# TensorE products that take their moving operand in 64-byte pieces from two halves, beside shifted tiles

## The chip, the cores and the metric

One core of one Trainium2 chip runs the whole program. The metric is the device time of one execution in microseconds (us). Terms used below: the PE is the matrix engine (TensorE); a product on it has a *stationary* operand of 128 x 128 weights, which a weight load (PEld in the profile) puts in place, and a *moving* operand of 128 partitions x 256 or 512 columns, which is streamed from SBUF past the weights; the result goes to PSUM. While one product streams, the weights of the next one are loaded. DVE, ACT and POOL are the vector, scalar and GpSimd engines.

## The reference

One encoder block over 512 tokens of width 2048, in float32. What matters here is that nearly all of it is matrix products:

```
proj  = rmsnorm(x) @ w_in                    # 512x2048 @ 2048x11280
...     # short convolution; hyena: two long convolutions by FFT (products with DFT tables)
...     # mLSTM, 4 heads, both directions, in chunks of 128
mixed = sigmoid(gate_a) * (y_a @ w_branch_a) + sigmoid(gate_b) * (y_b @ w_branch_b)
x     = x + mixed @ w_out                    # 512x2048 @ 2048x2048
gu    = rmsnorm(x) @ w_gate_up               # 512x2048 @ 2048x11264
x     = x + (silu(gu[:, :5632]) * gu[:, 5632:]) @ w_down
out   = rmsnorm(x)
```

## The kernel before, in words

Each float32 operand is split in two numbers of the type float32r: `h`, rounded, and `l`, the rest. One product of the reference becomes three on the PE (`mm3`): high by high, high by low, low by high. ACT makes `h` by a cast, DVE makes `l` by a subtraction (lines 74 to 80, 165 to 171, 1067 to 1072). All of these products go through one helper, `mm` (line 68), so the profile gives them one line, L69. The names in a row of the profile are output, then moving operand, then stationary operand: in `mm<-wh,h` the weights' high part `wh` is streamed and the activation's `h` is stationary; in `mm<-a,wh` it is the other way round. `mm` and `sd` are the two pools of PSUM tiles, four banks of 512 columns each.

The stages follow each other, with these products:

- To about 857 us: columns of `w_in` in groups (`group_feat`, 512 columns, moving operand `a`), with the hyena and mLSTM work in between (tiles `g` and `sg`, mostly 256 columns), and the values (`group_v`, 256 columns).
- To about 1157 us and again from about 1546 to 2402 us: the merge gates and the gate and up columns. These are Winograd (Strassen-like) products of 2 x 2 blocks: seven products of eight steps in place of eight, each step three products of 256 columns, so one column of blocks is 7 x 8 x 3 = 168 products. There are 16 + 44 = 60 such columns. The moving operands are halves of the tiles `a` or combinations `T`; the DVE forms the weights' sums `s`, and evacuates the results.
- From about 1157 to 1546 us: branch A (`ya`, tiles `a`), branch B (`yb`, tiles `y`), 384 products of 512 columns each, then the output projection, mostly with 512 columns.
- From about 2402 us: the down projection (`group_tok`), 512 columns, the weights moving and `h` stationary.

By the loops of the code there are 11,904 products of 256 columns: 60 x 168 = 10,080 in the Winograd columns, 4 x 192 = 768 for the values, 2 x 192 = 384 in the last two half groups of the output projection, 672 for the long convolutions. And 5,952 of 512 columns: 24 x 96 = 2,304 in feature groups, 32 for the gates, 768 in the branches, 3 x 192 = 576 for the output projection, 44 x 4 x 4 x 3 = 2,112 for the down projection, 96 for the mLSTM scores, 64 for the filters. The rest are transposes and small products.

The order of work on each engine is the order in which the code issues it (`drive` and `turns` interleave the streams by fixed rates). Tiles live in pools that are stacked from the left and from the right end of SBUF, so a pool's size sets the address of what is stacked after it. Most tiles are 2048 bytes in each partition; the tiles `g` are 2 x 258 words and so start at many distances. On the left come the small constants (`cp`), the weights (`wp`), the activations `a` (`ap`) and later `ts`, `pg`, the `w2...` pools and the tiles of the down projection; on the right `pr`, then `sx`, the `wm...` pools, `py` (tiles `y`) and `tp` (tiles `T` of the gate and up columns).

Of the kernel before, what the change touches and what calls it, by code (L numbers as in the profile page):

```python
# [8 lines left out]
F32 = mybir.dt.float32  # L9
# [6 lines left out]
P = 128  # L16
# [18 lines left out]
def hybrid_block_kernel(ctx, tc, x, norm1_w, w_in, conv_w, conv_b, filt_w1, filt_b1, filt_freq1,  # L35
# [6 lines left out]
    def new(pool, tag, shape=(P, L), dt=F32):  # L42
        n_tile[0] += 1
        return pool.tile(list(shape), dt, tag=tag, name=f"{tag}_{n_tile[0]}")
# [7 lines left out]
    cp = ctx.enter_context(tc.tile_pool(name="cp", bufs=1))  # L52
    wp = ctx.enter_context(tc.tile_pool(name="wp", bufs=1))
    wpool = [wp]
    WB = [4]
    ap_cm = tc.tile_pool(name="ap", bufs=32)
    ap = ap_cm.__enter__()
# [7 lines left out]
    def sd_ps():  # L65
        return new(psd, "sd")

    def mm(o, a, b, start, stop):
        nc.tensor.matmul(o, a, b, start=start, stop=stop)  # L69

    def mm3(o, aH, aL, bH, bL, start, stop):
        mm(o, aH, bH, start, False)
        mm(o, aH, bL, False, False)
        mm(o, aL, bH, False, stop)
# [44 lines left out]
    def dram(name, shape=(P, L)):  # L119
        return dp.tile(list(shape), F32, tag=name, name=name)  # L120
# [44 lines left out]
    def split_w(src, shape):  # L165
        n_tile[0] += 1
        h = wpool[0].tile(shape, F32R, tag="wh", name=f"wh_{n_tile[0]}", bufs=WB[0])
        l = wpool[0].tile(shape, F32R, tag="wl", name=f"wl_{n_tile[0]}", bufs=WB[0])
        nc.scalar.copy(h, src)  # L169
# [374 lines left out]
    h2 = {}  # L544
# [431 lines left out]
    def stream_a():  # L976
        yield from gate_rows()
        yield from need("filter")
        for kind, n in (("hy", 0), ("hy", 1), ("hd", 0), ("hy", 2), ("hy", 3)):
            yield from hyena(n) if kind == "hy" else mlstm(n)  # L980
        ph_cm.__exit__(None, None, None)
        ts_pool.append(ts_cm.__enter__())
        done.add("ts")
        for h in (1, 2, 3):
            yield from mlstm(h, h + 1)

    def stream_b():
        yield from filter_net()
        done.add("filter")
        yield from spectra()  # L990
        yield from need("ts")
        yield from combos_x()

    def turns(*streams):


        streams = [[s, 0] for s in streams]
        while streams:
            for _ in range(len(streams)):
                s = streams.pop(0)  # L1000
                if s[1] > tick[0]:
                    streams.append(s)
                    continue
                r = next(s[0], "end")
                if r == "pause":
                    s[1] = tick[0] + PAUSE
                if r != "end":
                    streams.append(s)
                if not isinstance(r, str):
                    break  # L1010
            else:
                r = "wait"
            if streams:
                yield r
# [139 lines left out]
    side = turns(stream_b(), stream_a())  # L1154
# [35 lines left out]
        return sx.tile(list(shape), F32, tag="bt", name=f"bt_{n_tile[0]}", bufs=4)  # L1190

    wm_cm = {t: tc.tile_pool(name="wm" + t, bufs=b, side="right", reuse_waits="tile") for t, b in (("r", 4), ("s", 6), ("h", 2), ("l", 2))}
    wm = {t: cm.__enter__() for t, cm in wm_cm.items()}
    d_g = [[dram(f"d_g{k}_{b}") for b in range(16)] for k in range(2)]

    def wtile(tag, shape, dt, bufs):
# [37 lines left out]
            nc.scalar.activation(C[j], C[j], AF.Sigmoid)  # L1234
            nc.gpsimd.dma_start(dst[j], C[j])

    for t in ("l", "h", "s", "r"):
        wm_cm[t].__exit__(None, None, None)
    ts_cm.__exit__(None, None, None)
    pg_cm = tc.tile_pool(name="pg", bufs=20, reuse_waits="tile")  # L1240
# [124 lines left out]
    for c in range(3):  # L1365
# [10 lines left out]
    hs = ctx.enter_context(tc.tile_pool(name="hs", bufs=3, reuse_waits="tile"))  # L1376
    w2_cm = {t: tc.tile_pool(name="w2" + t, bufs=b, reuse_waits="tile")
             for t, b in (("tb", 7), ("s2", 6), ("ta", 7), ("r2", 4), ("h2", 1), ("l2", 1))}
    w2 = {t: cm.__enter__() for t, cm in w2_cm.items()}

    def wt2(tag, shape, dt):
        return new(w2[tag], tag, shape, dt)
# [29 lines left out]
            nc.vector.tensor_tensor(U[j], U[j], G[j], ALU.mult)  # L1412
            nc.gpsimd.dma_start(d_h[f + j], U[j])

    for cm in reversed(list(w2_cm.values())):
        cm.__exit__(None, None, None)
    tp_cm.__exit__(None, None, None)
    sx_cm.__exit__(None, None, None)
# [48 lines left out]
    for c in range(4):  # L1467
        t = new(xq, "xst")
# [14 lines left out]
    for tb in range(4):  # L1483
        ts = slice(tb * P, (tb + 1) * P)
        for c in range(4):
# [3 lines left out]
            t = x2[tb][c]  # L1489
# [7 lines left out]
        for c in range(4):  # L1497
            t = x2[tb][c]
# [64 lines left out]
```

## Time and profile before

| | |
|---|---|
| median of 3 runs | 2893.94 us (2892.57 to 2894.06) |
| profiled execution | 2893.9 us, its span 2892.2 us |
| PE busy | 2864.4 us (99%), 18,412 products |
| weight loads (PEld) busy | 2593.9 us (90%) |
| DVE busy | 2107.6 us (73%) |
| ACT busy | 1271.4 us (44%) |
| DMA | 377.01 MB, 130 GB/s |

How to read it: PE rows have one record for each product, from its start to its modelled end. A new product starts before the one ahead has left the array, so records overlap: a 512-column product has a record of about 390 ns, while one starts every 227 ns or so. The price of a product is therefore the distance between starts, or the length of a stretch with nothing but products divided by their count. The chain of waits in order of time gives such stretches: start, length, line and count.

### The profile page before, as it was taken

How to read it: one execution, taken by the hardware profiler on the slowest of the kernel's cores; microseconds unless marked ns; L12 is line 12 of the kernel's file. 1: busy time of each engine (PE TensorE's matmuls, PEld its weight loads, DVE VectorE, ACT ScalarE, POOL GpSimd, SP SyncE). 2: the span in 40 equal slices, each digit the busy share in tenths (PEclk: the TensorE clock that was granted, in tenths of full speed). 3: DMA queues.
4: the chain of work that ended last, by engine and by line, in shares of the span. 5: the costliest groups of instructions: out<-in, count | busy, mean ns of one | idle time of the engine just before them, and what ended most of it. 6: DMA issues, size and time to landing. Idle time of an engine off the chain costs nothing.

```text
span 2892.2 us, 48205 instructions
## 1 busy us (share of the span) xinstructions
PE 2864.4 (99%) x18412; PEld 2593.9 (90%) x18412; DVE 2107.6 (73%) x3844; ACT 1271.4 (44%) x2265; POOL 187.6 (6%) x431
## 2 busy tenths in 40 slices
PE   9999999999999999999999999999999999999998
PEld 7788887888889999888899999999999998888886
DVE  7897978789578888554549888898888985233336
ACT  5434354346645455222435444444444445233224
POOL 0101011112200001000110000000000000000000
PEclk9999999999999999999999999999999999999999
DMA  5334333334444444743443433343343336343333
GB/s 179 110 121 128 120 117 124 117 118 145 132 146 128 131 142 139 247 139 95 152 148 109 130 120 114 120 125 118 117 128 114 118 110 207 96 131 117 124 114 127
DMA packets 285589, 377.01 MB, mean 130 GB/s; under 512 B 18620, under 2 KB 222852, under 8 KB 285357
## 3 DMA queue, kind: packets, MB, share of 16 engines
q1 hardware_dynamic: 261339, 298.36, 33.2%
q0 software_dynamic: 22752, 73.44, 7.5%
q8 instruction: 144, 2.36, 0.3%
q10 hardware_dynamic: 1266, 2.13, 0.2%
q14 instruction: 88, 0.72, 0.1%
HBM read 326.67 MB, written 47.20 MB: 129 GB/s over the span
## 4 chain that ended last, share of the span: by engine, by line
PE 82%; DVE 2%; DMA 1%; issue 0%; ACT 0%; POOL 0%; DVEq 0%; POOLq 0%; ACTq 0%
PE mm L69 58%; PE sd L69 23%; DMA wr<-in_w_down_dram 0%; PE sd L1326 0%; DMA d_v<-st 0%; DMA g<-d_hy 0%; DVE h L80 0%; DVE T L1354 0%; PE sd L724 0%; DVE wl L170 0%; DVE s L1087 0%; PE sd L963 0%; ACT h L79 0%; ACT wh L169 0%; PE sd L835 0%
## 5 line engine op out<-in xcount | busy, mean ns | idle before, releaser
L170 DVE TENSOR_TENSOR wl<-wr,wh 128x512 fp32r<-128x512 f32 x512 | 350.5, 688 | 461.5 <-ACT wh L169 456.6
L169 ACT CAST wh<-wr 128x512 fp32r<-128x512 f32 x512 | 316.8, 621 | 755.3 <-PE mm L69 692.6
L69 PE MATMUL mm<-a,wh 128*128 128x512 f32 (+1 forms) x2128 | 621.8, 375 | 0.0
L69 PEld LDWEIGHTS mm<-a,wh 128*128 128x128 f32 x2128 | 385.8, 189 | 68.3 <-issue 3.2
L69 PE MATMUL mm<-T,wh 128*128 128x256 f32 x2232 | 402.4, 282 | 2.6 <-ACT T L1353 2.2
L69 PE MATMUL sd<-T,wh 128*128 128x256 f32 x2224 | 399.1, 282 | 0.0
L69 PE MATMUL mm<-a,wl 128*128 128x512 f32 (+1 forms) x1064 | 398.1, 375 | 0.0
L69 PE MATMUL mm<-wh,h 128*128 128x512 f32 x1280 | 394.4, 389 | 1.1 <-ACT h L79 1.1
L69 PEld LDWEIGHTS mm<-T,wh 128*128 128x128 f32 x2232 | 343.5, 190 | 3.3 <-ACT T L1353 2.5
L69 PEld LDWEIGHTS sd<-T,wh 128*128 128x128 f32 x2224 | 341.5, 189 | 0.0
L1070 ACT CAST wh<-s 128x512 fp32r<-128x512 f32 x365 | 226.4, 621 | 255.2 <-PE sd L69 124.1
L69 PE MATMUL mm<-T,wl 128*128 128x256 f32 x1116 | 313.0, 280 | 0.3 <-DVE wl L1071 0.3
L69 PE MATMUL sd<-T,wl 128*128 128x256 f32 x1112 | 311.5, 280 | 0.0
L69 PEld LDWEIGHTS mm<-wh,h 128*128 128x128 f32 x1280 | 240.2, 188 | 51.2 <-ACT h L79 1.3
L69 PE MATMUL mm<-wh,a 128*128 128x256 f32 (+1 forms) x1152 | 260.6, 319 | 0.0
L1071 DVE TENSOR_TENSOR wl<-s,wh 128x512 fp32r<-128x512 f32 x365 | 249.5, 685 | 11.5 <-ACT wh L1070 9.7
L69 PE MATMUL mm<-wl,h 128*128 128x512 f32 x640 | 249.0, 389 | 0.0
L69 PEld LDWEIGHTS mm<-a,wl 128*128 128x128 f32 x1064 | 200.9, 189 | 34.7 <-issue 0.2
L69 PEld LDWEIGHTS mm<-T,wl 128*128 128x128 f32 x1116 | 212.1, 190 | 0.5 <-DVE wl L1071 0.5
L69 PEld LDWEIGHTS sd<-T,wl 128*128 128x128 f32 x1112 | 211.1, 190 | 0.0
L69 PEld LDWEIGHTS mm<-wh,a 128*128 128x128 f32 x1152 | 193.0, 190 | 15.3 <-issue 0.2
L69 PE MATMUL mm<-wl,a 128*128 128x256 f32 (+1 forms) x576 | 183.3, 318 | 0.0
(368 smaller groups left out, 4811.4 us busy)
## 6 DMA issues: line engine op xcount, KB each, us to landing
wr<-in_w_in_dram SPq DMA_DIRECT2D x140, 512.0 KB, 3.7
r<-in_w_gate_up_dram SPq DMA_DIRECT2D x100, 512.0 KB, 4.5
wr<-in_w_down_dram SPq DMA_DIRECT2D x88, 512.0 KB, 3.6
wr<-in_w_gate_up_dram SPq DMA_DIRECT2D x76, 512.0 KB, 4.0
r<-in_w_in_dram SPq DMA_DIRECT2D x36, 512.0 KB, 4.4
wr<-in_w_out_dram SPq DMA_DIRECT2D x32, 512.0 KB, 3.9
d_h<-xo POOLq DMA_DIRECT2D x44, 256.0 KB, 2.6
hl<-d_h SPq DMA_DIRECT2D x44, 256.0 KB, 3.6
```

What stands on the lines that cost most here:

```text
L69: nc.tensor.matmul(o, a, b, start=start, stop=stop)
L169: nc.scalar.copy(h, src)
L170: nc.vector.tensor_tensor(l, src, h.bitcast(F32), ALU.subtract)
L1070: nc.scalar.copy(h, a)
L1071: nc.vector.tensor_tensor(l, a, h.bitcast(F32), ALU.subtract)
```

## The change

`mm` now rewrites both the output and the moving operand of each product of 256 or 512 columns whose operands have two dimensions: `lines` reads the tile as two halves (`h`), each in pieces of 16 words (64 bytes), and orders them piece by piece: the first piece of the left half, the first of the right half, the second of the left half, and so on. The output is written in the same order, so each result lands where it did. Products of 258 columns, transposes and smaller ones are as before.

Beside that it puts spare tiles that nothing uses into the stacks of pools: 32 words (128 bytes) on the left behind `wp`, 24 words (96 bytes) at the right end, 32 words between the `wm` pools `s` and `h`, and 32 words between `r2` and `h2` of the `w2` pools. They shift what is stacked after them.

```
+    def shift(name, words, **kw):
+        cm = tc.tile_pool(name=name, bufs=1, **kw)
+        ctx.enter_context(cm).tile([P, words], F32, tag=name, name=name)
+
+    def shifted(name, words, **kw):
+        cm = tc.tile_pool(name=name, bufs=1, **kw)
+        cm.__enter__().tile([P, words], F32, tag=name, name=name)
+        return cm
...
+    shift("left", 32)
+    shift("right", 24, side="right")
...
+    def lines(v):
+        return v.rearrange("p (h c e) -> p c h e", h=2, e=16)
+
     def mm(o, a, b, start, stop):
+        if o.shape[-1] in (256, 512) and len(o.shape) == 2 and len(b.shape) == 2:
+            o, b = lines(o), lines(b)
         nc.tensor.matmul(o, a, b, start=start, stop=stop)
...
-    wm = {t: cm.__enter__() for t, cm in wm_cm.items()}
+    wm = {t: wm_cm[t].__enter__() for t in ("r", "s")}
+    wm_cm["x"] = shifted("wmx", 32, side="right")
+    wm.update({t: wm_cm[t].__enter__() for t in ("h", "l")})
...
-    for t in ("l", "h", "s", "r"):
+    for t in ("l", "h", "x", "s", "r"):
...
-    w2 = {t: cm.__enter__() for t, cm in w2_cm.items()}
+    w2 = {t: w2_cm[t].__enter__() for t in ("tb", "s2", "ta", "r2")}
+    h2_cm = shifted("h2x", 32)
+    w2.update({t: w2_cm[t].__enter__() for t in ("h2", "l2")})
...
-    for cm in reversed(list(w2_cm.values())):
+    for cm in (w2_cm["l2"], w2_cm["h2"], h2_cm, *(w2_cm[t] for t in ("r2", "ta", "s2", "tb"))):
```

By the addresses that the tiles get, the distance modulo 256 bytes from a product's moving operand to the weights that are loaded while it streams (those of the next product) is as follows:

| columns | products | before | after |
|---|---|---|---|
| 256 | 11,904 | 5,587 at 224, 5,102 at 0, 939 at 32, 276 at others | 11,266 at 128, 638 at others |
| 512 | 5,952 | 5,334 at 0, 441 at 224, the rest at others | 5,512 at 128, the rest at others |

The instructions of every engine and their order stay as they were. On the PE, in the down projection, the rows of before:

```order
L69 MATMUL mm_29386<-wh_29561,h_28822 128x512
L69 MATMUL mm_29387<-wh_29561,h_28821 128x512
L69 MATMUL mm_29387<-wl_29562,h_28821 128x512
L69 MATMUL mm_29387<-wh_29561,h_28822 128x512
L69 MATMUL mm_29388<-wh_29561,h_28821 128x512
```

and the same place now (line 88 is the helper's product in the changed file; a tile's number only counts what was made before it):

```order
L88 MATMUL mm_29404<-wh_29579,h_28840 128x16x2x16
L88 MATMUL mm_29405<-wh_29579,h_28839 128x16x2x16
L88 MATMUL mm_29405<-wl_29580,h_28839 128x16x2x16
L88 MATMUL mm_29405<-wh_29579,h_28840 128x16x2x16
L88 MATMUL mm_29406<-wh_29579,h_28839 128x16x2x16
```

Nothing moved; the shape of the output is 16 pieces x 2 halves x 16 words in place of 512 words.

## The prediction

> **What bounds the kernel now.** I read the page first, then who the PE waited for, then the chain of waits in order of time, then single products in the timeline. From the page: the span, the busy time of each engine, the granted clock in 40 slices.
>
> ```profile
> span 2892.2 us, 48205 instructions
> PE 2864.4 (99%) x18412; PEld 2593.9 (90%) x18412; DVE 2107.6 (73%) x3844; ACT 1271.4 (44%) x2265; POOL 187.6 (6%) x431
> PEclk9999999999999999999999999999999999999999
> ```
>
> The PE is never without work for long and its clock is granted in full. A busy PE is not yet a PE at its peak, so the question is what a product costs. The two longest sums that the PE waited for another engine or a transfer, from the list of waits:
>
> ```profile
> PE sd L288 <- DMA xt<-in_x_dram: 6.9, 2, 3.9
> PE mm L69 <- ACT T L1353: 2.2, 1, 2.2
> ```
>
> Some 20 us of waits in all: a kernel that is its products, one behind the other. The chain in order of time gives their spacing, because long stretches of it are products alone (start us, length us, count):
>
> ```profile
> 1077.07 20.00 PE mm L69 x168
> 1156.98 220.22 PE mm L69 x960
> 1469.78 23.04 PE mm L69 x192
> 1605.84 19.88 PE mm L69 x168
> 1625.72 19.88 PE sd L69 x168
> 2402.15 413.86 PE mm L69 x1824
> ```
>
> The x168 rows are one Winograd column each, 256-column products: 19.88 / 168 = 118.3 ns from one to the next, in the earlier stage 20.00 / 168 = 119.0. The x1824 row is the down projection, 512-column products: 413.86 / 1824 = 226.9 ns. The same row of the code (L69) thus costs 118.3 and 226.9 ns for 256 and 512 columns. If both follow a fixed part plus a price per column, the price is (226.9 - 118.3) / 256 = 0.424 ns, and the fixed part 118.3 - 256 x 0.424 = 9.7 ns. That is an estimate: it assumes one fixed part for both widths. 9.7 ns over all 11,904 + 5,952 products is 173 us, 6% of the span: the pot that this change can reach for.
>
> Is this part fixed by nature, or by where the operands lie? Two stretches with the same instruction, the same shape and the same stream of weights tell. In the timeline, branch A (moving operand `a`) and branch B (moving operand `y`); first column the start in us:
>
> ```profile
> 1200.82 0.39 PE L69 MATMUL mm<-a,wl 128*128 128x512 f32 x1
> 1201.05 0.61 PE L69 MATMUL mm<-a,wh 128*128 128x512 f32 x2
> 1201.50 0.39 PE L69 MATMUL mm<-a,wl 128*128 128x512 f32 x1
> 1201.73 0.61 PE L69 MATMUL mm<-a,wh 128*128 128x512 f32 x2
> 1202.18 0.39 PE L69 MATMUL mm<-a,wl 128*128 128x512 f32 x1
> ```
> ```profile
> 1310.16 0.40 PE L69 MATMUL mm<-y,wl 128*128 128x512 f32 x1
> 1310.39 0.63 PE L69 MATMUL mm<-y,wh 128*128 128x512 f32 x2
> 1310.86 0.40 PE L69 MATMUL mm<-y,wl 128*128 128x512 f32 x1
> 1311.09 0.63 PE L69 MATMUL mm<-y,wh 128*128 128x512 f32 x2
> 1311.56 0.40 PE L69 MATMUL mm<-y,wl 128*128 128x512 f32 x1
> ```
>
> Three products take 0.68 us with `a` and 0.70 us with `y`: some 6.7 ns more each. The windows row of 80 us inside each branch says it again, 354 products against 345 (the count behind PE busy):
>
> ```profile
> 1160.00:1240.00 80.00, 80.00 (x354) 66.25 (x353) 39.74 (x62) 22.84 (x39) 1.62 (x3) 1.00 0.65 223
> 1250.00:1330.00 80.00, 80.00 (x345) 64.41 (x344) 46.42 (x71) 24.76 (x43) 0.00 (x0) 1.00 0.42 132
> ```
>
> What differs is the address: `a` begins at the same place modulo 256 bytes as the weights being loaded, `y` 224 bytes on. The DMA share is higher in the faster stretch, so transfers aren't the cause. So a product's time depends on how the addresses of the streamed operand and of the loading weights stand to each other: the two reads hinder each other, and at least a part of the 9.7 ns is that. The 192 products of 23.04 us above, 120.0 ns each, and the 118.3 of the gate and up columns are the same at 256 columns: one shape, several prices. Both were laid out without regard to this, so no row shows a pair that is wholly out of each other's way.
>
> **The change part by part.** *What it moves.* Nothing on any engine: each keeps its instructions, their order and their waits, but for the number of a DMA lane. The spare tiles (128 bytes at left, 96 at right, 128 in two inner places) hold no data and cost no instruction. Now 11,266 of the 11,904 products of 256 columns and 5,512 of the 5,952 of 512 find the operand 128 bytes (modulo 256) from the next product's weights; before, nearly all stood at 0 or at 32 bytes to either side.
>
> *What the pieces do.* The operand is read 64 bytes here, 64 bytes half a tile on. Both halves are a multiple of 256 bytes apart, so the address modulo 256 goes forward only 64 bytes in 32 columns, 32 x 0.424 = 13.6 ns. A weight load reads 512 bytes; at that pace it takes 8 x 13.6 = 109 ns. Its pace isn't in the trace directly, but in the 256-column stage the load engine has no gap:
>
> ```profile
> 1600.00:2400.00 800.00, 800.00 (x6763) 800.00 (x6762) 711.15 (x1245) 383.23 (x644) 21.75 (x41) 1.00 0.38 118
> ```
>
> PEld is busy 800.00 of 800, one load for each product of 118.3 ns, so a load is done in 118.3 ns or less. If it paces at about 109 ns, both reads walk at one speed, and a distance of 128 in 256 bytes, once set, is kept through the whole load: they never meet. Before, the stream walked at twice that speed and passed the load again and again, whatever the start.
>
> *The gain.* For a product at distance 128 it lies between 0 and the 9.7 ns, below nothing if the jumps cost something (a rival). The spread that addresses alone make, 6.7 ns at 512 columns, shows that the greater part of such a cost can come and go, so I take the upper end less 1 ns for what may be fixed: 8.7 ns x (11,266 + 5,512) = 146.0 us. The 384 products with `y` also lose their 6.7 ns: 2.6 us.
>
> *What is given back.* The 638 + 441 products at other distances may now walk in step with a load in the same place. Their bounds are 0 and something like the worst pair seen, 6.7 ns; I take the latter: 7.2 us. Then the engine that feeds the PE: in the row above the DVE is busy 711.15 us of 800, 89%. At 109.6 ns a product the stage lasts 800 x 109.6 / 118.3 = 741 us, and the DVE has 96% of it. It stays the smaller of the two, but the splits, sums and evacuations come in a fixed order and some will be late. The nearest row is the first stage:
>
> ```profile
> 0.00:857.00 857.00, 844.60 (x4587) 714.75 (x4588) 686.32 (x1365) 406.57 (x753) 109.68 (x287) 1.00 0.42 130
> ```
>
> There the DVE has 80% and the PE lacks work for 12.4 us, 1.4%. The 60 Winograd columns take 60 x 18.4 = 1,105 us after the change; 1% of it, 11 us, is my estimate (bounds 0 and 40 us, if waits of 3.5% come). The down stage has no such neighbour. Transfers stay hidden: the DMA engines' share (the last column but one) is 0.42 and 0.38 in these rows, and 0.44 at most in a span 4.5% shorter.
>
> *The sum.* 146.0 + 2.6 - 7.2 - 11 = 130.4 us. The profiled execution took 2893.9 us (span 2892.2 us and 1.7 us around it), the median of the runs is 2893.94, so no correction: 2893.9 - 130.4 = **2763.5 us**. All of the 9.7 ns and nothing given back would be 2893.9 - 162.7 - 2.6 = 2728.6; half of the 9.7 ns with the same losses 2893.9 - 81.4 - 2.6 + 18.2 = 2828. That is this case's own range, with some room below for the estimate of 9.7: 2720 to 2828.
>
> **The rivals.** *The load is the bound at 256 columns.* PEld without a gap for 800 us would also be seen if the load itself needed 118 ns and the stream waited for it. Then only 512-column products gain: 5,512 x 8.7 + 2.6 = 50.6 us, less 441 x 6.7 = 3.0: 2846 us. For it: that row. Against it: 119.0, 118.3 and 120.0 ns for the same load in different places. Chance 0.17.
>
> *The jumps cost.* The result goes to PSUM in the same 64-byte pieces, and the stream jumps at each: 32 times in a 512-column product, 16 times in one of 256, together 5,952 x 32 + 11,904 x 16 = 380,928 times. If each jump costs the time of one column, 0.424 ns, that is 161.5 us: 2763.5 + 161.5 = 2925 us, slower than before even with the collisions gone; it decides from 130.4 / 380,928 = 0.34 ns a jump. No product of before has a moving operand or a result in pieces, so no row speaks against it. The Trainium skill (PSUM — Partial Sum Buffer, Specifications) says that PSUM has lines of 8 bytes and that any access pattern that isn't contiguous slows matmuls significantly; taken to the letter this is the rival's rule. Here each piece is contiguous over 64 bytes, and the price hangs on whether the jump or the broken line costs; the trace shows neither. Chance 0.12.
>
> *Nothing to win.* If the loads don't touch the stream's reads at all, the 9.7 ns is the price of changing weights and stays: 2894 us. The Trainium skill (TensorE: Matmul & The Clock Gate, Step-by-step: what each phase is for) says that the PE has two independent read ports and that loading the next weights doesn't steal read bandwidth from the running matmul. By that rule the two branches should cost alike; the measured 226.7 and 233.3 ns (0.68 and 0.70 us for three) speak against it. Chance 0.05.
>
> *In step, but together.* If a load starts some 27 ns (two steps of 64 bytes) off the stream's start, distance 128 becomes distance 0, and they collide all the way. Priced by the worst pair seen: 16,778 x 6.7 = 112 us, 3006 us. Against it, a product and the next one's load in the timeline, which start together to 10 ns:
>
> ```profile
> 1499.82 0.28 PE L69 MATMUL mm<-wh,a 128*128 128x256 f32 x1
> 1499.82 0.19 PEld L69 LDWEIGHTS mm<-wl,a 128*128 128x128 f32 x1
> ```
>
> Chance 0.03.
>
> **How the numbers follow.** The forecast has 0.63, the rivals the rest. The likeliest case gives 2763.5 us. The range from 2720 to 2880 holds it and the load-bound case, 0.80 together, and ends short of no change. Faster by over 0.2% (5.8 us, about what a measurement of this kernel can tell from none): 0.63 + 0.17 = 0.80; within it 0.05; slower 0.12 + 0.03 = 0.15.
>
> **What would show it right or wrong.** Right: x168 rows of the chain near 18.4 us in place of 19.88, the down stage's x1824 near 398 us (218.2 ns each), no difference between `a` and `y`, and the PE's new waits on `wl`, `s` or `T` of the DVE in the Winograd stages, below 20 us. Load-bound: down stage shorter, x168 rows still 19.88. Jumps: both rows longer, the 512-column product by twice as much as the 256. Nothing to win: `a` and `y` keep their difference or only that goes. The forecast is wrong if the x168 rows stay above 19.2 us, half of the gain.

## The result and the profile after

The changed kernel takes 2975.77 us (median of 4 runs, 2973.80 to 2977.39), the kernel before beside it 2894.0 us: a ratio of 1.0283, 95% interval 1.0267 to 1.0300. It is slower by 82 us, where 130 us less were forecast. The profiled execution's span went from 2892.2 to 2972.1 us, 79.9 us more.

The first rows of the page after:

```profile
span 2972.1 us, 48219 instructions
PE 2949.0 (99%) x18412; PEld 2629.4 (88%) x18412; DVE 2116.8 (71%) x3844; ACT 1270.0 (43%) x2265; POOL 186.1 (6%) x431
PEclk9999999999999999999999999999999999999999
```

The number of products is the same, the clock is still granted in full, and DVE and ACT are busy for the same time as before to within 10 us. The PE's longest waits stay what they were:

```profile
PE sd L307 <- DMA xt<-in_x_dram: 6.7, 3, 4.0
PE mm L88 <- ACT T L1374: 2.3, 1, 2.3
```

So no wait took the gain; the products themselves got longer. The chain shows it, in order of time (start us, length us, count):

```profile
880.67 20.16 PE sd L88 x168
1183.07 230.40 PE mm L88 x960
1415.22 46.09 PE mm L88 x192
1607.47 20.16 PE mm L88 x168
2455.29 507.17 PE mm L88 x2112
```

The down projection is 507.17 / 2112 = 240.1 ns a product (before 226.9), a Winograd column 20.16 / 168 = 120.0 ns (before 118.3 and 119.0). The branches are 230.40 / 960 = 240.0 ns. The difference between `a` and `y` has gone, but to a price above both; 80 us inside branch A and inside branch B now hold 335 products each (before 354 and 345):

```profile
1190.00:1270.00 80.00, 80.00 (x335) 63.34 (x334) 36.55 (x57) 20.49 (x35) 0.54 (x1) 1.00 0.62 210
1280.00:1360.00 80.00, 80.00 (x335) 63.34 (x334) 45.32 (x70) 24.71 (x42) 0.00 (x0) 1.00 0.41 131
```

Where the 79.9 us lie: the first Winograd column began at 857.39 us before, which is this row of its chain,

```profile
857.39 20.00 PE sd L69 x168
```

and at 880.67 now, so the first stage costs 23.3 us more. The branches begin at 1183.07 in place of 1156.98, another 2.8 us. The down projection begins at 2455.29 in place of 2402.15: 27.1 us more in between, of which 44 columns x 0.28 us = 12.3 us are gate and up. From there to the end it is 516.8 in place of 490.05 us, 26.8 more. The 512-column products are a third of all and carry most of the loss.

### The profile page after: what moved, and what is told of

It is laid out like the page before. It is cut to its first block, busy times and chain, and to the rows that moved or that the text cites. A ratio compares the mean times of both kernels' runs of the same rounds, so it can differ in the third digit from the quotient of the medians.

```text
span 2972.1 us, 48219 instructions
## 1 busy us (share of the span) xinstructions
PE 2949.0 (99%) x18412; PEld 2629.4 (88%) x18412; DVE 2116.8 (71%) x3844; ACT 1270.0 (43%) x2265; POOL 186.1 (6%) x431
## 4 chain that ended last, share of the span: by engine, by line
PE 83%; DVE 1%; issue 0%; ACT 0%; DMA 0%; POOL 0%; DVEq 0%; ACTq 0%; POOLq 0%
PE mm L88 59%; PE sd L88 23%; PE sd L1347 0%; DMA g<-d_hy 0%; DVE T L1375 0%; PE sd L743 0%; PE sd L982 0%; DVE wl L189 0%; DVE s L1106 0%; PE sd L854 0%; ACT g L363 0%; DVE g L643 0%; DVE g L767 0%; DVE g L787 0%; DVE pp L383 0%
## 5 line engine op out<-in xcount | busy, mean ns | idle before, releaser
L88 PE MATMUL mm<-a,wh 128*128 128x512 f32 (+1 forms) x2128 | 644.0, 386 | 0.0
L88 PE MATMUL mm<-wh,h 128*128 128x512 f32 x1280 | 411.8, 403 | 1.1 <-ACT h L98 1.1
L88 PE MATMUL mm<-a,wl 128*128 128x512 f32 (+1 forms) x1064 | 409.1, 385 | 0.0
L88 PE MATMUL mm<-wl,h 128*128 128x512 f32 x640 | 258.0, 403 | 0.0
L88 PEld LDWEIGHTS mm<-wh,a 128*128 128x128 f32 x1152 | 192.9, 189 | 19.2 <-issue 0.3
```

## The experiments

The expectations speak of theories by letters. **J**: each jump between pieces costs two column times, 0.83 ns, whatever the load does. **C**: stream and load, now at one speed, collide all the way (the prediction's rival "in step, but together"). Later come **K**: half of the extra time is the load's and half the jumps'; **R**: any read in pieces runs at one fixed rate; **W**: the price is for starting a piece, wherever it lies; **A**: the price is for leaving the order of addresses.

They count with 0.417 ns a column. That is an estimate from the output projection of before, where 192 products took 43.55 us with 512 columns and 23.04 us with 256:

```profile
1379.03 43.55 PE mm L69 x192
```

By it, 512 columns need some 213.3 ns and 256 some 106.7, so J gives 213.3 + 32 x 0.83 = 240 and 106.7 + 16 x 0.83 = 120 ns, and the fixed part of a contiguous product comes to some 13 ns (13.3 in the expectations) in place of the prediction's 9.7.

### Which part: placement, pieces, read, write

**Placement alone** (e1): the two lines in `mm` that call `lines` are taken out of the changed kernel.

```
-        if o.shape[-1] in (256, 512) and len(o.shape) == 2 and len(b.shape) == 2:
-            o, b = lines(o), lines(b)
```

> The shifted tiles alone; operand and output contiguous as before. Theory J (each jump between 64-byte pieces costs about two column times, 0.83 ns, whatever the load does): no jumps, so a 512-column product is back near 226.7 ns and one of 256 near 118 to 120, the branch with y no longer apart from a; 2880 to 2900 us. Theory C (the products of the changed kernel are slow because stream and load, now at one speed, collide all the way): the stream again passes the load, same numbers, 2880 to 2900 us. If placement at 128 alone removes or adds collisions, the 512-column spacing moves from 226.7 towards 217 or 233 ns and the time by up to 60 us either way.

Measured: 2916.03 us against 2892.8, ratio 1.0083 (1.0066 to 1.0100). The distance of 128, which was to keep the two reads apart, costs 23 us by itself. In its chain the branches and the down projection:

```profile
1161.66 223.28 PE mm L86 x960
1614.97 19.93 PE mm L86 x168
2413.52 424.14 PE mm L86 x1824
```

The down projection's products take 424.14 / 1824 = 232.5 ns (226.9 before), the columns 19.93 / 168 = 118.6 ns (118.3). So the third reading in the expectation came true, on the losing side. By the code, the spare tile behind `wp` moves the streamed `a` in branch A and leaves the loading weights where they were; in the down projection it moves the loading `h` and leaves the streamed weights. Both come to some 232.5 ns, which speaks for the distance between the two, not for the place of the moving operand alone.

**Pieces alone** (e2): `lines` and the two lines in `mm` put into the kernel before, no spare tiles.

> The pieces alone, at the addresses of before (distance 0 or 224 for nearly all). J: the price is the jump's, so 240 and 120 ns as in the changed kernel, 2975 us give or take 10. C: the distance decides whether they collide all the way, so the spacing differs clearly from 240 and 120 ns: the products at 0 (a, h) against those at 224 (y, T) differ by 5 ns or more.

Measured: 2977.61 us (one run), 507.16 / 2112 = 240.1 ns, and the branches 230.40 us for 960, 240.0 ns, at distance 0 as at 224:

```profile
1183.85 230.40 PE mm L74 x960
1609.40 20.21 PE mm L74 x168
2459.19 507.16 PE mm L74 x2112
```

With pieces the distances 0, 224 and 128 cost the same at 512 columns (at 256, 20.21 / 168 = 120.3 ns against 120.0), so C falls, and the rival "in step, but together" with it. Placement and pieces do not add up (23 and 85 us alone, 82 us together): the pieces' price replaces what the address made.

**Pieces in the read alone** (e3) and **in the write alone** (e4), both with the shifted tiles:

```
-            o, b = lines(o), lines(b)
+            b = lines(b)          # e3
+            o = lines(o)          # e4
```

> Shifted tiles and pieces in the moving operand alone; the output is written contiguously, so its columns land in another order (the result is a permuted one). If the jump costs in the read: still 240 and 120 ns, 2975 us. If it costs in the write to PSUM: the reads are in step with the load at distance 128 and have no price of their own, so 214 to 218 ns and 107 to 110 ns, near 2764 us (the forecast). C: as in the changed kernel, 240 and 120 ns, 2975 us.

> Shifted tiles and pieces in the output alone; the moving operand is read contiguously (columns land in another order, the result is a permuted one). If the jump costs in the write: at least 240 and 120 ns, up to 253 and 133 ns where the old fixed part of 13 ns comes on top, 2975 to 3200 us. If it costs in the read, or C: as in the run with placement alone, 2880 to 2900 us.

Measured: 3001.45 us with the read in pieces, 2917.18 us with the write in pieces, one run each. The chain of e3, then of e4:

```profile
1043.45 20.16 PE sd L88 x168
1184.57 230.40 PE mm L88 x960
1611.51 20.72 PE mm L88 x168
2482.85 507.29 PE mm L88 x2112
```
```profile
1162.14 223.35 PE mm L88 x960
1616.55 19.94 PE mm L88 x168
2415.10 424.14 PE mm L88 x1824
```

The write in pieces costs nothing: e4's rows are those of placement alone (424.14 both). The price is in the read. The rule of the Trainium skill (PSUM — Partial Sum Buffer, Specifications), by which any access pattern that isn't contiguous slows matmuls, does not hold for pieces of 64 bytes: 232.5 ns with and without them. The read in pieces with a contiguous write is even dearer in the gate and up columns, 20.72 / 168 = 123.3 ns against 120.0 with both in pieces, and so e3's time lies 26 us above the 2975 us that were expected. In the merge gates, also 256 columns wide, it stays at 20.16 / 168 = 120.0. Why is open; a contiguous write alone isn't the reason, as f1 below has one and 120.0 ns in both stages.

### Is it the load, and what does a jump cost?

**Pieces of 128 bytes** (e5), `e=32` in `lines`; **another order** (e7), every second 64-byte piece first:

```
-        return v.rearrange("p (h c e) -> p c h e", h=2, e=16)
+        return v.rearrange("p (h c e) -> p c h e", h=2, e=32)    # e5
+        return v.rearrange("p (c h e) -> p h c e", h=2, e=16)    # e7
```

> The changed kernel with pieces of 128 bytes: half as many jumps. Theory J (a jump in the read costs 0.83 ns, two column times, and nothing else of the product's time is left to the load): 16 and 8 jumps, 213.3 + 13.3 = 226.7 ns at 512 columns and 113.3 ns at 256, unless collisions with the load, now out of step, come back on top (up to 240 and 120 ns); 2800 to 2900 us. Theory K (half of the extra time in the changed kernel is the load's, half the jumps', one column time each): 213.3 + 13.3 + 6.7 = 233 ns and 117 to 120 ns, 2890 to 2940 us.

> The changed kernel with 64-byte pieces in another order: every second piece from start to end, then the others; the jumps are 64 bytes long instead of half a tile, and the read again goes forward at more than the load's speed. J: as many jumps, the same price, 240 and 120 ns, 2975 us, if collisions stay hidden; up to 253 and 133 ns if they come back. If the price is that of a far jump (between halves): back to 227 to 233 ns and 119 ns, 2890 to 2920 us.

Measured: e5 2955.93 us and 20.16 us a column (120.0 ns), with this row for the down projection, 431.97 / 1824 = 236.8 ns:

```profile
2443.66 431.97 PE mm L88 x1824
```

e7 took 2974.84 us, 507.17 / 2112 = 240.1 ns and 120.0 ns. A jump of 64 bytes costs as much as one of half a tile, as J says; but half as many jumps save 3.3 ns of a 512-column product, not 13.3, and none of a 256-column one. J's size falls; K's 233 ns is missed too.

**Half of the load**: in every product that neither starts nor ends a sum, 64 weight columns (and output partitions) in place of 128. In the kernel before (e8) and in the changed one (e9):

```
     def mm(o, a, b, start, stop):
+        if not (start or stop) and len(a.shape) == 2 and a.shape[-1] == P and o.shape[-1] in (256, 512) and len(o.shape) == 2:
+            a, o = a[:, 0:64], o[0:64]
```

> The kernel before, with 64 in place of 128 weight columns (and output partitions) in every product that neither starts nor ends a sum: half of the result's rows miss most of their terms; the streams and their addresses are unchanged, the loads are half as long. If the fixed part of 13.3 ns in each product of before is made by the load's reads: near half of it, 220 ns at 512 columns and 110 to 114 ns at 256, about 2780 us. If it is a price of changing weights: unchanged, 226.7 and 118 to 120 ns, 2894 us.

> The same halving of the loads in the changed kernel. J: the jumps set the time, so 240 and 120 ns stay, 2975 us. K: the load's half of the extra time is halved, 227 to 234 ns and 113 to 117 ns, 2830 to 2900 us.

Measured: e9 2974.29 us, with the branches at 230.40 us for 960 and 20.16 us a column, as in the changed kernel to the last digit: with pieces the length of the load sets nothing, so K falls. e8: 2873.76 us, and its chain holds the first surprise about the kernel before:

```profile
1459.66 21.82 PE mm L71 x192
1611.69 19.55 PE sd L71 x168
2375.38 419.72 PE mm L71 x1824
```

A 256-column product of the gate and up columns falls from 118.3 to 19.55 / 168 = 116.4 ns, and one of the output projection's last half groups from 120.0 to 21.82 / 192 = 113.6 ns; but one of 512 columns rises from 226.9 to 419.72 / 1824 = 230.1 ns. At 512 columns the fixed part that the prediction put down to the load's reads doesn't halve with the load; at 256 it falls by 2 to 6 ns.

**Pieces of 32 and of 256 bytes** (e6 with `e=8`, e10 with `e=64`):

> The changed kernel with pieces of 32 bytes: twice as many jumps (64 and 32). Theory J (two column times, 0.83 ns, for each jump): 213.3 + 53.3 = 266.7 ns at 512 columns and 133.3 ns at 256, about 3290 us. Theory R (any read in pieces runs at a fixed rate, nine column times for eight columns, however long the pieces): 240 and 120 ns, 2975 us.

> The changed kernel with pieces of 256 bytes: 8 and 4 jumps. J: 6.7 and 3.3 ns of jumps on top of what the contiguous read has at this place (232 and 119 ns in the run with placement alone), so up to 239 and 122 ns, 2920 to 2990 us; if jumps and that part hide each other in part, 228 to 236 and 118 to 120 ns, 2890 to 2950 us. R: 240 and 120 ns.

Measured: 3032.13 us and 2926.47 us. The chain of e6, then of e10, which fell where its second reading had it (jumps and the contiguous part hide each other in part):

```profile
1614.57 20.72 PE sd L88 x168
2506.63 514.20 PE mm L88 x2112
```
```profile
1617.05 20.16 PE mm L88 x168
2424.55 424.13 PE mm L88 x1824
```

With the shifted tiles, the down projection's rows over their counts, and those of the gate and up columns:

| pieces | 512 columns, ns | 256 columns, ns |
|---|---|---|
| contiguous (e1) | 232.5 | 118.6 |
| 256 bytes (e10) | 232.5 | 120.0 |
| 128 bytes (e5) | 236.8 | 120.0 |
| 64 bytes (changed kernel) | 240.1 | 120.0 |
| 32 bytes (e6) | 243.5 | 123.3 |

J expected 266.7 ns with 32 bytes and R the same 240 for all: neither. From 256 bytes down the price at 512 columns grows by steps of 3.3 to 4.3 ns as pieces are halved, so it is no fixed price a piece: above the contiguous 232.5 ns it is 0.27, 0.24 and 0.17 ns for each of 16, 32 and 64 pieces. The 256-column prices hang on the stage too: with 256-byte pieces the merge gates stay at 118.6 ns.

**A new piece without distance** (e13): each piece begins with the word that the one ahead ended with. The result is made of 481 (241) different columns.

```
+    def overlapped(v):
+        n = v.shape[-1] // 16
+        return bass.AP(v.tensor, v.offset, [list(v.ap[0]), [15, n], [1, 16]])
...
+            b = overlapped(b)
```

> Shifted tiles; the moving operand in pieces of 16 words, each beginning with the word that the piece before ended with, so there are as many pieces but no distance between them; the output is contiguous. The columns read are 481 and 241 different ones in place of 512 and 256, so the result is not the reference's. If the price lies in starting a new piece as such: 240 and 120 to 123 ns, 2975 to 3000 us. If it lies in going to another place in memory: as contiguous, 232 and 119 ns, about 2917 us.

Measured: 2968.46 us, between the two readings. Its chain in the merge gates and in the gate and up columns:

```profile
1170.34 20.48 PE sd L89 x168
1614.64 19.79 PE mm L89 x168
```

At 512 columns the start of a piece costs without any distance, 510.36 / 2112 = 241.6 ns. At 256 columns the two stages part: 20.48 / 168 = 121.9 ns in the merge gates, above the 120.0 of the changed kernel, and 19.79 / 168 = 117.8 ns in the gate and up columns, below the contiguous 118.6. These pieces also begin at any word, not at every 64 bytes, so this run alone doesn't settle it.

**A piece twice** (f1), **half a tile twice** (f3), contiguous writes, shifted tiles:

```
+        return bass.AP(v.tensor, v.offset, [list(v.ap[0]), [16, v.shape[-1] // 32], [0, 2], [1, 16]])    # f1
+        return bass.AP(v.tensor, v.offset, [list(v.ap[0]), [0, 2], [1, v.shape[-1] // 2]])               # f3
```

> Shifted tiles; each 64-byte piece of the left half is streamed twice and the right half not at all (so the result is not the reference's); the output is contiguous. As many piece starts as in the changed kernel, but the second of each pair is the place just read, and the pairs follow each other in memory. Theory W (a new piece costs by its start, wherever it lies): 238 to 243 ns at 512 columns and 119 to 126 ns at 256, 2960 to 3000 us. Theory A (the price is for leaving the order of addresses, half of the starts here return to a place still at hand): clearly less, 225 to 236 ns at 512 columns, 2880 to 2945 us.

> Shifted tiles; the left half of each moving operand is streamed twice, contiguously, with a single step back between (the result is not the reference's). W and A alike: one new start, next to nothing: 232 and 119 ns as in the run with placement alone, 2905 to 2930 us. If instead any moving operand of more than one dimension is slow, 240 and 120 ns, 2975 us.

Measured: f1 2975.85 us, 507.17 / 2112 = 240.1 ns and 120.0 ns; f3 2916.57 us, 424.14 / 1824 = 232.5 ns and 118.7 ns, the numbers of placement alone. f1's chain:

```profile
1609.53 20.16 PE mm L88 x168
2457.36 507.17 PE mm L88 x2112
```

Half of f1's starts go back to the 64 bytes just read, and the rest goes on in order, and the price is that of the changed kernel. This is what W expects and not A: the price is for starting a piece, wherever it lies, and one start more (f3) costs nothing that shows. W says where the price arises, not how it comes about; the table shows that it isn't the same for each start.

**A quarter of the load** (f2): as e8, with 32 columns.

> The kernel before with 32 weight columns in every product that neither starts nor ends a sum (three quarters of the result's rows miss most of their terms). With 64 columns a 512-column product rose from 226.7 to 230.3 ns and one of 256 fell from 119.0 to 116.3 ns. If the load's reads make the fixed part of 13.3 ns of the contiguous products: now clearly under 222 ns and 112 ns, 2760 to 2830 us. If the fixed part belongs to the change of weights as such: 225 to 231 ns and 113 to 117 ns, 2840 to 2880 us.

Measured: 2892.19 us. Its windows row of 700 us in the gate and up columns, and its chain:

```profile
1650.00:2350.00 700.00, 700.00 (x5974) 649.87 (x5972) 630.76 (x1104) 338.88 (x570) 18.94 (x35) 1.00 0.38 120
```
```profile
1602.21 19.69 PE mm L71 x168
2391.05 422.65 PE mm L71 x1824
```

The loads did get shorter. Three rows of the groups of weight loads in the down projection, of the kernel before, of e8 and of f2, give the mean ns of one load behind its busy time: 188, 134 and 109.

```profile
L69 PEld LDWEIGHTS mm<-wl,h 128*128 128x128 f32 x640 | 120.1, 188 | 25.0
L71 PEld LDWEIGHTS mm<-wl,h 128*64 128x64 f32 x640 | 86.0, 134 | 58.9
L71 PEld LDWEIGHTS mm<-wl,h 128*32 128x32 f32 x640 | 69.6, 109 | 76.0
```

In the gate and up columns the loads now leave gaps (PEld 649.87 of 700 us, where it had none), and yet a product takes 422.65 / 1824 = 231.7 ns at 512 columns and 117.2 ns at 256. In the down projection, at distance 0, a quarter of the load makes a product 4.8 ns longer than the full load, and in the gate and up columns 1.1 ns shorter. In branch B, at distance 224, the 384 products with `y` go from 233.4 to 231.6 ns with half and 231.9 ns with a quarter (from their first to their last start, 89.4, 88.7 and 88.8 us). So at 512 columns the fixed part isn't the load's reads, but for some 1.5 ns at distance 224; at 256 columns a part of 1 to 6 ns goes with the load's length. The expectation's first reading is missed by far; the second, a price of changing weights as such, by little (2892 us against 2840 to 2880).

### A contiguous version, placed anew

**e12**: the kernel before, with two spare tiles that move `y` to distance 0 and the tiles `T` of the gate and up columns to 32.

```
+    yx_cm = shifted("yx", 56, side="right")
     py_cm = tc.tile_pool(name="py", bufs=16, side="right", reuse_waits="tile")
...
+    tx_cm = shifted("tx", 48, side="right")
     tp_cm = tc.tile_pool(name="tp", bufs=42, side="right", reuse_waits="tile")
```

> The kernel before, contiguous, with two spare tiles alone: y to distance 0 from the weights (from 224), the tiles T of the gate and up columns to 32 (from 224). If placement alone sets how a contiguous read and the load hinder each other, as the rows of before show: y's products fall from 233.3 to 226.7 ns (2.6 us in all), the 44 columns of 168 products from 118.3 to about 117 ns (9 us): 2878 to 2886 us, faster by 0.3 to 0.5%. If the distance modulo 256 isn't what counts: 2893 us, the same.

Measured: 2890.51 us against 2893.78, ratio 0.9980 (0.9970 to 0.9991); its chain:

```profile
1156.15 217.63 PE mm L74 x960
1602.83 19.88 PE mm L74 x168
```

The branches lose 220.22 - 217.63 = 2.6 us, just what `y`'s rows promised. The columns stay at 19.88 us: for `T` 32 is as good as 224, the 9 us don't come, and the range of 2878 to 2886 us is missed. Of the versions that compute the whole block it is the only one that beats both kernels, by 0.1 to 0.3%.

## Why the prediction was wrong

The bound was right: the kernel is its products, and the end follows their spacing; the prices of 118.3 and 226.9 ns and the difference of 6.7 ns between `a` and `y` are there, and e12 shows that `y`'s place makes the difference. Two steps failed, and both had to hold for a gain.

*The step from "addresses change the price" to "the fixed part is the load's reads, and reads that walk in step are free of it".* The prediction wrote that "the spread that addresses alone make ... shows that the greater part of such a cost can come and go", and booked 146.0 us. The quarter load speaks against it: with a quarter of the load's columns the 512-column product of the down projection doesn't fall at all (231.7 against 226.9 ns), and half of the load takes only 2 to 6 ns off one of 256 columns. And the distance of 128, taken for the one that is out of the load's way, is a worse one: by itself it makes 512-column products 5.6 ns longer (e1). That addresses have an effect was shown (e1, and the 2.6 us that e12 took off `y`); that the fixed part is of the same kind was argued. The rival "nothing to win", which had 0.05, was the nearer on this point, though not at 256 columns. The rule of the Trainium skill that stood there (TensorE: Matmul & The Clock Gate, Step-by-step: what each phase is for), that loading weights doesn't steal the running matmul's read bandwidth, fits the 512-column products of f2 (231.7 ns) and e9 (240.0 ns); it doesn't explain why an address changes a price, nor the 1.9 to 6.4 ns that half a load saves at 256 columns.

The pace of the load, on which the prediction's picture of "in step" rests, isn't what failed. It took from the row without a gap that a load is done in 118.3 ns or less; the record of one load is 188 ns, and records overlap. But 96 columns less shorten it by 188 - 109 = 79 ns, so by this estimate 128 columns take some 105 ns, near the 109 that it assumed.

*The pieces at nothing.* The forecast had no term for the read in pieces; it left the price to a rival with 0.12. Measured, it is 240.1 - 226.9 = 13.2 ns at 512 columns and 1.7 or 1.0 ns at 256 (where 120.0 ns are also the price of the worst contiguous columns before, 23.04 us for 192). The rival "the jumps cost" had the sign and, by chance, the size at 512 columns (32 x 0.424 = 13.6), but the wrong place: it blamed the write to PSUM, which e4 shows to be free, and a fixed price for each jump, which the table rules out. Its 2925 us also counted the gain that wasn't there; without it, it would be 3055, and 2975.77 was measured.

The rival "the load is the bound at 256 columns" falls too: with half or a quarter of the load the columns go only to 116.4 and 117.2 ns, and with pieces they rise to 120.0 whatever the load.

*Small terms.* The 7.2 us for products at other distances and the 11 us for a late DVE have no counterpart: with pieces the distance doesn't count (e2), and a slower PE waits less, not more. The PE's 12.4 us without work in the first 857 us became 880.00 - 871.19 = 8.8 us:

```profile
0.00:880.00 880.00, 871.19 (x4584) 722.69 (x4585) 688.59 (x1365) 406.84 (x753) 108.37 (x287) 1.00 0.40 126
```

So some of the first stage's longer products are hidden in time in which the PE had nothing to do.

*The forecast's own test* said that it is wrong if a column stays above 19.2 us; it went to 20.16. The pattern that the text gave for the jumps, the 512-column product longer by twice as much as the 256, was not met either: 13.2 ns against 1.7.

*Still open:* why the start of a piece costs what it does (3 to 4 ns more with each halving, far less at 256 columns), what the fixed part of a contiguous product is (10 to 13 ns by the two estimates), and why a distance of 128 costs 5.6 ns at 512 columns. A product without any weight load was not tried.

## What to carry to other kernels

A cost that addresses change is not thereby a cost that addresses can take away: measure what is left when the suspected cause is cut to a quarter before the whole of it is booked as gain. Keep the moving operand of a 512-column float32r product contiguous or in pieces of 256 bytes or more; with a contiguous read, the order of its output in PSUM was free at 64 bytes. Where two operands of one shape show two spacings, try the better one's place first, with the access pattern as it is.

## What the runs showed of the hardware that was not expected

- A product whose moving operand and output come in 64-byte pieces takes 120.0 to 120.3 or 240.0 to 240.1 ns here, at distances 0, 224 and 128 from the weights and with half of the load; streaming each piece twice in place gives the same (f1).
- Writing a product's output to PSUM in 64-byte pieces, in turn to the two halves of the tile, costs nothing when the read is contiguous (2917.18 against 2916.03 us).
- A shorter weight load made contiguous 512-column products at distance 0 longer: 226.9, 230.1 and 231.7 ns with 128, 64 and 32 weight columns, while the record of one load fell from 188 to 134 and 109 ns.
- Contiguous 512-column products took 226.9 ns with the moving operand at distance 0 from the loading weights, 232.5 ns at 128 and 233.3 ns at 224 (before and e1).
